# Other prices in a build-time scheduler's clock, and a sample's cached keys loaded in transposed form

## The chip, the cores and the metric

The kernel runs on one core of a Trainium2 chip. A core has five engines with instruction streams of their own: TensorE (PE, matrix products; its weight loads, PEld, overlap with them), VectorE (DVE), ScalarE (ACT), GpSimd (POOL) and SyncE (SP), which here issues every DMA. Each engine runs its stream in the order in which it was built, and waits on semaphores where it needs another's result. Matrix products are written to PSUM, everything else lies in SBUF, and DMAs move data between SBUF and device memory (DRAM). The metric is the device time of one execution in microseconds (us); lower is better.

## What is computed

One layer of a streaming encoder, in fp32, for 2048 frames of a new stream ("prompt") and 64 frames of a running one ("sample") with 4096 cached keys and values:

```python
h = rmsnorm(x, norm_g) @ w_in                     # 1024 -> 6144 columns
qa, ka, va, za, qb, kb, vb, zb, ga, gb = split(h)
qa = rmsnorm(qa.reshape(B, T, 4, 2, 64), qn_g)     # q and k: RMS norm per 64 columns
ka = rmsnorm(ka.reshape(B, T, 4, 2, 64), kn_g)
# branch A, differential attention; cache: (1, 1, 4096, 4 heads, 2, 64)
s = einsum('bqhcd,bkhcd->bhcqk', q, k) * 64 ** -0.5 - slopes * dist   # then the chunk mask
p = softmax(s);  a = p[:, :, 0] - lam * p[:, :, 1];  oa = a @ v
# branch B: retention, 4 heads, chunks of 64, a state carried on
m = sigmoid(ga) * ((rmsnorm(oa) * silu(za)) @ w_oa) + sigmoid(gb) * ((rmsnorm(ob) * silu(zb)) @ w_ob)
y = x + m @ w_out
```

For the sample, the keys are the cached ones followed by the 64 new ones. Outputs are y, the new k and v, and the retention states.

## The kernel before

**Products in three parts.** An fp32 operand is split in a high part rounded to fp32r (an ACT copy) and a low part (operand less high part, a DVE or POOL subtraction). A product is then three matmuls: high with high, high with low, low with high. In `mm_group` (L385) these are the matmuls of the input projection.

**Two streams of work.** `w_stream` makes the projections in two halves of 1024 prompt frames, the first with the sample's 64. Column groups of 256 columns follow each other. For each, `w_load` and `w_split` bring and split the weights (L355 on ACT, L362 on POOL), and `natural` (for v, k and q) runs one group of 24 matmuls for each tile of 128 frames into a PSUM tile `mm` (two buffers), then starts a task for what follows. For q and k that task is `fin_qk`: ACT copies the tile to `raw` (L418) and squares it into a `tlo` buffer (L419), DVE sums the squares (L424) and makes the mean (L426), ACT and DVE make the reciprocal root (`rsqrt_small`, L220 to L230), DVE multiplies `raw` (L434, and L438 for k), PE transposes the result (L451), ACT and DVE split it (L461 to L467), and DMAs store it. `raw`, `thi` and `tlo` have two buffers each. The other columns (`transposed`) are evacuated by `fin_t` (L551).

`z_stream` does attention and retention on what is stored. In `attn_head`, `qk_block` makes scores (L725, L726) and adds the bias on DVE (L734), `softmax` takes exponentials on ACT (L764) and combines the two rows on DVE (L785), and `at_pv` transposes the rows on PE (L832), splits them (L845, L847) and multiplies by v (L810 to L812). Between the two halves comes `sample_attn`. For each head and each 512 cached keys, it takes a loaded tile `kn`, has PE transpose it in four pieces into the PSUM tile `at` (L922), splits it (L933 on ACT, L935 on DVE) into `ath` and `atl`, and runs three matmuls (L892 to L894). The loader `s_loader` queues eight key tiles (`K`, four buffers) and nine value tiles (`V`, four buffers) for each head. After both streams, `out_stream` makes the output products (L1303 to L1305, L1368 to L1370).

**The planner.** All these functions are generators. While the kernel is built, `loop` resumes whichever is ready with the best priority, and what it then emits goes to the ends of the engines' streams; so the order on PE, ACT, DVE and the DMA queue is fixed by this loop. It keeps a clock for each engine. `P(cycles)` moves PE's, which is also the loop's present time; `A(n)`, `V(n)` and `G(n)` add an operation of n elements to ACT's, DVE's and POOL's and return when its result is there (`LAT`, 250 ns, later); `ld` does it for DMAs (bytes/300 ns + 2600 ns). A generator that yields a time is resumed when PE's clock has come there, one that yields a function when this is true. `take` and `give` hand out buffers with the times at which they come free. The clock decides only the order; on the chip the semaphores hold whatever was placed too early. The prices before the change are these:

```python
self.pe += cycles / 2.4 + 2.5                                  # P
self.act = max(self.act, ready) + 0.9 * n + 60 + extra         # A
self.dve = max(self.dve, ready) + rate * n + 65                # V, rate 1.05
self.pool = max(self.pool, ready) + 2.4 * n + 100              # G
```

Of the kernel before, what the change touches and what calls it, by code (L numbers as in the profile page):

```python
# [8 lines left out]
F32 = mybir.dt.float32  # L9
# [12 lines left out]
PAST = 4096  # L22
# [32 lines left out]
class Hybrid:  # L55
# [55 lines left out]
        self.res[tag].free += [t] * k  # L111

    def P(self, cycles):
        self.pe += cycles / 2.4 + 2.5
        return self.pe + LAT

    def A(self, n, ready=0.0, extra=0.0):
        self.act = max(self.act, ready) + 0.9 * n + 60 + extra
        return self.act + LAT

    def V(self, n, ready=0.0, rate=1.05):
        self.dve = max(self.dve, ready) + rate * n + 65
        return self.dve + LAT

    def G(self, n, ready=0.0):
# [148 lines left out]
    def x_norm(self, j, xt, jk, gn, t, tg, r, seg, col, left):  # L274
        nc = self.nc
        yield t
        ss, ms, y = (self.sp.tile([128, 1], F32, tag=k, name=k)[:r] for k in ("x_ss", "x_ms", "x_y"))
        nc.scalar.activation(jk[:r], xt, AF.Square, accum_out=ss)
        t = self.A(1024, self.pe, 270)
        yield t  # L280
        nc.scalar.activation(y, ss, AF.Ln, scale=1.0 / D, bias=self.epst[:r])
        nc.scalar.activation(y, y, AF.Exp, scale=-0.5)
        self.A(1, t, 140)
        t2 = self.A(1, 0, 140)
        nc.vector.tensor_scalar(ms, ss, 1.0 / D, EPS, op0=ALU.mult, op1=ALU.add)
        self.V(1, t)
        yield t2
        nc.vector.scalar_tensor_tensor(out=ms, in0=y, scalar=y, in1=ms, op0=ALU.mult, op1=ALU.mult)
        nc.vector.tensor_scalar(ms, ms, -0.5, 1.5, op0=ALU.mult, op1=ALU.add)
        nc.vector.tensor_mul(y, y, ms)  # L290
        for _ in range(3):
            t = self.V(100, t2)
        if tg > self.pe:
            yield tg
        nc.vector.scalar_tensor_tensor(out=xt, in0=xt, scalar=y, in1=gn[:r], op0=ALU.mult, op1=ALU.mult)
        self.xq[j] = (xt, self.V(1150, t), r, seg, col)
        left[0] -= 1

    def x_tile(self, j):
# [561 lines left out]
    def sample_attn(self):  # L861
        nc = self.nc
# [8 lines left out]
        for h in range(4):  # L871
            yield from self.take("q")
            qt = self.sb(ap, [128, 4, 256], "q", dt=F32R)
            qq = [qt[:, j, 0:128] for j in range(2)]
            for j in range(2):
                nc.vector.memset(qq[j].bitcast(F32), 0.0)
                t = self.V(128)
            yield t
            for j in range(2):
                for c in range(2):  # L880
                    tq = self.ld(qq[j][64 * c:64 * c + 64, 64 * c:64 * c + 64].bitcast(F32),
                                 self.qT[j][h, 64 * c:64 * c + 64, T:TT], 1 << 14)
            yield from self.take("row", 4)
            units = [self.row() for _ in range(4)]
            tail = sp.tile([128, 64], F32, tag="s_tail", name="s_tail", bufs=2)
            accs = sp.tile([128, 16], F32, tag="s_acc", name="s_acc", bufs=3)

            def mms(m, n, kh, kl, t):
                yield max(t, tq, tb)
                yield from self.take("s")  # L890
                ps = self.psum("s")[:, :n]
                nc.tensor.matmul(ps, qq[0], kh, start=True, stop=False)  # L892
                nc.tensor.matmul(ps, qq[0], kl, start=False, stop=False)
                nc.tensor.matmul(ps, qq[1], kh, start=False, stop=True)  # L894
                for _ in range(3):
                    t = self.P(max(n, 256))
                self.give("ath", t)
                self.give("atl", t)
                acc = accs[:, m:m + 1]
                out = units[m // 2][:, (m % 2) * 512:(m % 2) * 512 + 512] if m < 8 else tail  # L900
                tab = base[:, 0:512] if m < 8 else base[:, 512:576]
                nc.vector.tensor_tensor_reduce(
                    out=out, in0=ps, in1=tab, scale=-SLOPES[h], scalar=3.0e38,
                    op0=ALU.add, op1=ALU.min, accum_out=acc)
                t = self.V(n, t)
                if m < 7:
                    nc.vector.tensor_scalar_add(acc, acc, 512.0 * (7 - m) * SLOPES[h])
                    self.V(1)
                self.give("s", t)
                yield self.pe  # L910

            todo = None
            for m in range(9):
                n = 512 if m < 8 else 64
                if m < 8:
                    yield lambda: len(self.kns) > 0
                    kn, t = self.kns.pop(0)
                    yield t
                    yield from self.take("at")
                    tp = self.psum("at")  # L920
                    for k in range(4):
                        nc.tensor.transpose(tp[:, 128 * k:128 * k + 128], kn[:, k, :], self.ident)  # L922
                        t = self.P(256)
                    self.give("K", t)
                if todo is not None and not self.has("ath", "atl"):
                    yield from mms(*todo)
                    todo = None
                yield from self.take("ath")
                yield from self.take("atl")
                kh = self.sb(ap, [128, 512], "ath", dt=F32R)[:, :n]  # L930
                kl = self.sb(ap, [128, 512], "atl", dt=F32R)[:, :n]
                if m < 8:
                    nc.scalar.copy(kh, tp)  # L933
                    t = self.A(512, t)
                    nc.vector.tensor_sub(kl, tp, kh.bitcast(F32))  # L935
                    t = self.V(512, t)
                    self.give("at", t)
                else:
                    self.ld(kh.bitcast(F32), self.kT[0][h, :, T:TT], 1 << 15)
                    t = self.ld(kl.bitcast(F32), self.kT[1][h, :, T:TT], 1 << 15)  # L940
                yield self.pe
                if todo is not None:
                    yield from mms(*todo)
                todo = (m, n, kh, kl, t)
            yield from mms(*todo)
            self.give("q", self.pe + LAT)
            mx = sp.tile([128, 9], F32, tag="s_mx", name="s_mx", bufs=3)
            nc.vector.tensor_reduce(mx[:, 7:8], accs[:, :9], axis=AX.X, op=ALU.min)
            t = self.V(16, t)
            for m in range(7):  # L950
                nc.vector.tensor_scalar_add(mx[:, m:m + 1], mx[:, 7:8], -512.0 * (7 - m) * SLOPES[h])
                t = self.V(1)
            yield t
            lp = sp.tile([128, 16], F32, tag="s_lp", name="s_lp", bufs=3)
            nc.scalar.activation(tail, tail, AF.Exp, bias=mx[:, 7:8], scale=-1.0, accum_out=lp[:, 8:9])
            self.A(64, t, 220)
            te = []
            for m in range(8):
                u = units[m // 2][:, (m % 2) * 512:(m % 2) * 512 + 512]
                nc.scalar.activation(u, u, AF.Exp, bias=mx[:, m:m + 1], scale=-1.0, accum_out=lp[:, m:m + 1])  # L960
                te.append(self.A(512, t, 220))
            self.spawn(self.sample_pv(h, units, tail, te, lp, oall), 2, "z")
# [14 lines left out]
    def s_loader(self):  # L977
        for h in range(4):
            for m in range(8):
                yield from self.take("K")  # L980
                kn = self.sb(self.ap, [128, 4, 128], "K", "kn")
                t = self.ld(kn, self.i["cache_k_diff"][0, 0, 512 * m:512 * m + 512, h]
                            .rearrange("(t p) c d -> p t (c d)", p=128), 1 << 18)
                self.kns.append((kn, t))
                yield self.pe
            for m in range(9):
                yield from self.take("V")
                vc = self.sb(self.ap, [128, 4, 128], "V", "vc")
                if m < 8:
                    t = self.ld(vc, self.i["cache_v_diff"][0, 0, 512 * m:512 * m + 512, h]  # L990
                                .rearrange("(t p) e -> p t e", p=128), 1 << 18)
                else:
                    t = self.ld(vc[:64, 0, :], self.vsN[:, 128 * h:128 * h + 128], 1 << 15)
                self.vcs.append((vc, t))
                yield self.pe
# [596 lines left out]
```

## Time and profile before

| | us |
|---|---|
| median of three runs | 2158.24 |
| lowest and highest of them | 2155.09, 2160.27 |
| the profiled execution | 2151.0 |
| its span, first to last instruction | 2149.2 |
| mean granted TensorE clock | 0.984 of full speed |

The profile is of one execution. A row by engine and stretch gives the stretch's length, the busy time of each engine with its count of instructions, the granted TensorE clock (PEclk, 1.00 is full speed), the busy share of the DMA engines and GB/s. A row of a group gives line, engine, operation, the tile written and the tiles read, shapes and count; then busy time, mean ns of one, the engine's idle time just before such instructions, and which instruction ended that idle time. A row of the list of waits gives who waited for whom, us in total, times, and the longest. Matmuls overlap in the array, so a matmul's own duration is longer than the distance from one start to the next.

### The profile page before, as it was taken

The page shows a single profiled execution, that of the slowest core. Times are in us where ns is not written, and L with a number is a line of the kernel's source. Part 1 is how long each engine was busy: PE and PEld are TensorE (multiplying, and loading weights), DVE is VectorE, ACT ScalarE, POOL GpSimd, SP SyncE. Part 2 cuts the span into 40 slices and gives each one's busy share as a digit, 9 for nine tenths or more (in the row PEclk, how much of TensorE's full clock was granted, in tenths as well). Part 3 has the DMA queues.
Part 4 walks back from the last instruction along what each step waited for, and adds up shares of the span by engine and source line. Part 5 has one row for each costly group of instructions (what it writes and reads, how often), then busy time and mean ns, then how long its engine had stood idle before and what let it go on. Part 6 is the DMA issues. An engine that isn't in the chain of part 4 may idle for free.

```text
span 2149.2 us, 36945 instructions
## 1 busy us (share of the span) xinstructions
PE 2050.0 (95%) x13152; PEld 1853.5 (86%) x13152; DVE 1011.6 (47%) x2957; ACT 1006.9 (47%) x2349; POOL 462.6 (22%) x428
## 2 busy tenths in 40 slices
PE   7978999999999999988989999999999978999999
PEld 6977899989899999978879988888888867998897
DVE  6265856544311200455886756624642335454442
ACT  5333766644434422534765656644654334333221
POOL 1111112110122421110211121233123423222210
PEclk8999999999999999999999999999999989999999
DMA  6654444346545542455343252453233545444431
GB/s 206 189 144 124 136 137 128 112 122 171 156 120 133 159 140 84 130 152 152 94 133 110 70 147 87 136 165 94 64 96 115 172 144 185 134 143 146 135 115 60
DMA packets 363145, 281.66 MB, mean 131 GB/s; under 512 B 67408, under 2 KB 342480, under 8 KB 362960
## 3 DMA queue, kind: packets, MB, share of 16 engines
q1 hardware_dynamic: 362960, 279.30, 43.9%
q8 instruction: 104, 1.70, 0.3%
q14 instruction: 81, 0.66, 0.1%
HBM read 187.71 MB, written 91.49 MB: 130 GB/s over the span
## 4 chain that ended last, share of the span: by engine, by line
PE 48%; DVE 2%; DMA 1%; ACT 1%; issue 1%; SPq 0%; POOL 0%; POOLq 0%; DVEq 0%; ACTq 0%
PE mm L385 20%; PE at L1368 3%; PE at L1370 3%; PE at L1369 3%; PE at L832 2%; PE s L725 2%; PE s L726 2%; PE s L1304 1%; PE s L1303 1%; PE mm L1304 1%; PE mm L1303 1%; PE mm L1305 1%; PE s L1305 1%; PE pv L812 1%; PE pv L811 1%; PE pv L810 1%
## 5 line engine op out<-in xcount | busy, mean ns | idle before, releaser
L385 PE MATMUL mm<-xh,wh 128*128 128x512 f32 (+2 forms) x1280 | 466.2, 364 | 3.4 <-ACT ev L551 2.4
L385 PE MATMUL mm<-xh,wl 128*128 128x512 f32 (+2 forms) x1280 | 452.2, 353 | 0.3 <-POOL wl L362 0.3
L385 PE MATMUL mm<-xl,wh 128*128 128x512 f32 (+2 forms) x1280 | 451.8, 353 | 0.0
L362 POOL TENSOR_TENSOR wl<-ws,wh 128x512 fp32r<-128x512 f32 x190 | 252.0, 1346 | 771.6 <-ACT wh L355 562.9
L385 PE MATMUL mm<-wh,xh 128*128 128x256 f32 x1088 | 320.9, 295 | 11.8 <-ACT sq L419 6.9
L385 PE MATMUL mm<-wl,xh 128*128 128x256 f32 x1088 | 311.0, 286 | 1.1 <-POOL wl L362 0.8
L385 PE MATMUL mm<-wh,xl 128*128 128x256 f32 x1088 | 310.6, 285 | 0.2 <-DVE xl L317 0.2
L385 PEld LDWEIGHTS mm<-xh,wh 128*128 128x128 f32 x1280 | 241.9, 189 | 36.2 <-issue 3.4
L385 PEld LDWEIGHTS mm<-xl,wh 128*128 128x128 f32 x1280 | 242.0, 189 | 31.8 <-issue 3.4
L385 PEld LDWEIGHTS mm<-xh,wl 128*128 128x128 f32 x1280 | 241.4, 189 | 31.7 <-POOL wl L362 0.8
L385 PEld LDWEIGHTS mm<-wh,xh 128*128 128x128 f32 x1088 | 207.9, 191 | 19.1 <-ACT sq L419 9.9
L385 PEld LDWEIGHTS mm<-wl,xh 128*128 128x128 f32 x1088 | 208.2, 191 | 4.3 <-POOL wl L362 1.2
L385 PEld LDWEIGHTS mm<-wh,xl 128*128 128x128 f32 x1088 | 207.7, 191 | 0.4 <-DVE xl L317 0.4
L551 ACT COPY ev<-mm 128x512 f32<-128x512 f32 x140 | 71.3, 510 | 278.4 <-PE mm L385 230.3
L847 DVE TENSOR_TENSOR atl<-at,ath 128x512 fp32r<-128x512 f32 (+1 forms) x144 | 93.9, 660 | 145.3 <-ACT ath L845 145.0
L764 ACT ACTIVATE row<-row,a_mx 128x1024 f32<-128x1024 f32 (+7 forms) x160 | 153.3, 962 | 15.3 <-DVE a_mx L744 15.3
L734 DVE CUSTOM_DVE_ANT_0 row<-s,dfar 128x512 f32<-128x512 f32 (+2 forms) x192 | 117.8, 631 | 62.0 <-PE s L726 52.6
L845 ACT CAST ath<-at 128x512 fp32r<-128x512 f32 (+1 forms) x144 | 79.5, 562 | 112.2 <-PE at L832 111.6
L355 ACT CAST wh<-ws 128x512 fp32r<-128x512 f32 x192 | 116.1, 619 | 27.4 <-PE mm L385 21.7
L725 PE MATMUL s<-K,q 128*128 128x512 f32 (+3 forms) x320 | 122.8, 388 | 5.3 <-DVE a_acc L734 5.2
L609 POOL TENSOR_TENSOR r_y<-r_y,r_sq 128x256 f32<-128x256 f32 x33 | 29.5, 894 | 426.6 <-DVE r_sq L606 368.2
L726 PE MATMUL s<-K,q 128*128 128x512 f32 (+3 forms) x320 | 116.3, 365 | 0.0
(202 smaller groups left out, 4199.0 us busy)
## 6 DMA issues: line engine op xcount, KB each, us to landing
ws<-in_w_in_dram SPq DMA_DIRECT2D x192, 256.0 KB, 3.0
q<-qT SPq DMA_DIRECT2D x128, 128.0 KB, 2.9
V<-vN SPq DMA_DIRECT2D x24, 512.0 KB, 5.1
K<-kT SPq DMA_DIRECT2D x48, 256.0 KB, 3.8
gt<-gaT SPq DMA_DIRECT2D x64, 132.0 KB, 2.1
gt<-gbT SPq DMA_DIRECT2D x64, 132.0 KB, 2.2
xt<-in_x_prompt_dram SPq DMA_DIRECT2D x16, 512.0 KB, 5.1
kn<-in_cache_k_diff_dram SPq DMA_DIRECT2D x32, 256.0 KB, 3.5
```

The costliest lines, as they stand in the source:

```text
L355: nc.scalar.copy(h, st)
L362: nc.gpsimd.tensor_sub(l, st, h.bitcast(F32))
L385: nc.tensor.matmul(ps, p, q, start=c == 0 and i == 0, stop=c == KC - 1 and i == 2)
L551: nc.scalar.copy(ev, ps)
L725: nc.tensor.matmul(ps, q1s, kk, start=True, stop=False)
L726: nc.tensor.matmul(ps, q2s, kk, start=False, stop=True)
L734: nc.vector.tensor_tensor_reduce(out=units[k0 // 1024][:, k0 % 1024:k0 % 1024 + n], in0=ps, in1=tab, scale=-SLOPES[h], scalar=3.0e38, op0= ...
L764: nc.scalar.activation(u, u, AF.Exp, bias=mx, scale=-1.0, accum_out=lp[:, k:k + 1])
L845: nc.scalar.copy(ah[:, :w], at[:, :w])
L847: nc.vector.tensor_sub(al[:, :w], at[:, :w], ah[:, :w].bitcast(F32))
L1368: nc.tensor.matmul(ps, h, wh[:, nsl], start=ct == 0, stop=False)
L1369: nc.tensor.matmul(ps, h, wl[:, nsl], start=False, stop=False)
```

## The change

The prices of PE, ACT and DVE in the clock are changed, with the `extra` amounts and element counts in `x_norm` that stood beside the old ones. POOL's price, the DMAs' and `LAT` stay. The cached keys come to the kernel in a second layout, made by the host before the launch (head, channel, key): a tile of 512 keys is loaded as 128 partitions of 512 consecutive values, and is split from SBUF. The four transposes, the `at` tile and its give and take fall away; `K` is given back after the subtraction instead of after the transposes.

```diff
@@ P, A, V
-        self.pe += cycles / 2.4 + 2.5
+        self.pe += cycles / 2.4 + 13.0
...
-        self.act = max(self.act, ready) + 0.9 * n + 60 + extra
+        self.act = max(self.act, ready) + 0.84 * n + 165 + extra
...
-        self.dve = max(self.dve, ready) + rate * n + 65
+        self.dve = max(self.dve, ready) + rate * n + 155
@@ x_norm
-        t = self.A(1024, self.pe, 270)
+        t = self.A(1024, self.pe, 190)
...
-        self.A(1, t, 140)
-        t2 = self.A(1, 0, 140)
+        self.A(1, t, 40)
+        t2 = self.A(1, 0, 40)
...
-            t = self.V(100, t2)
+            t = self.V(20, t2)
...
-        self.xq[j] = (xt, self.V(1150, t), r, seg, col)
+        self.xq[j] = (xt, self.V(1100, t), r, seg, col)
@@ sample_attn
                     yield t
-                    yield from self.take("at")
-                    tp = self.psum("at")
-                    for k in range(4):
-                        nc.tensor.transpose(tp[:, 128 * k:128 * k + 128], kn[:, k, :], self.ident)
-                        t = self.P(256)
-                    self.give("K", t)
...
-                    nc.scalar.copy(kh, tp)
+                    nc.scalar.copy(kh, kn)
                     t = self.A(512, t)
-                    nc.vector.tensor_sub(kl, tp, kh.bitcast(F32))
+                    nc.vector.tensor_sub(kl, kn, kh.bitcast(F32))
                     t = self.V(512, t)
-                    self.give("at", t)
+                    self.give("K", t)
@@ s_loader
-                kn = self.sb(self.ap, [128, 4, 128], "K", "kn")
-                t = self.ld(kn, self.i["cache_k_diff"][0, 0, 512 * m:512 * m + 512, h]
-                            .rearrange("(t p) c d -> p t (c d)", p=128), 1 << 18)
+                kn = self.sb(self.ap, [128, 512], "K", "kn")
+                t = self.ld(kn, self.i["cache_k_T"][h, :, 512 * m:512 * m + 512], 1 << 18)
@@ kernel
+    k = given.pop("cache_k_diff")[0, 0]
+    given["cache_k_T"] = np.ascontiguousarray(k.transpose(1, 2, 3, 0).reshape(4, 128, PAST))
```

## The prediction

> **What bounds the kernel now.** First the page's busy times, then busy time by stretch of the span.
>
> ```profile
> span 2149.2 us, 36945 instructions
> PE 2050.0 (95%) x13152; PEld 1853.5 (86%) x13152; DVE 1011.6 (47%) x2957; ACT 1006.9 (47%) x2349; POOL 462.6 (22%) x428
> ...
> core 0: us, PE busy (x) PEld busy (x) DVE busy (x) ACT busy (x) POOL busy (x), PEclk, DMA share, GB/s
> 0.00:60.00 60.00, 46.07 (x311) 43.15 (x312) 34.35 (x89) 32.77 (x80) 5.64 (x9) 0.86 0.61 196
> 90.00:180.00 90.00, 71.04 (x539) 67.93 (x538) 52.66 (x179) 31.05 (x110) 13.47 (x11) 0.94 0.49 140
> 180.00:260.00 80.00, 72.21 (x543) 65.95 (x542) 59.41 (x246) 47.74 (x141) 11.48 (x9) 1.00 0.46 127
> 260.00:880.00 620.00, 615.41 (x4102) 566.18 (x4102) 207.93 (x628) 282.64 (x637) 132.28 (x110) 1.00 0.47 133
> 880.00:1000.00 120.00, 105.32 (x820) 100.43 (x819) 62.49 (x190) 50.99 (x147) 20.28 (x16) 0.99 0.51 151
> 1000.00:1150.00 150.00, 135.66 (x970) 126.35 (x969) 120.45 (x378) 96.93 (x233) 19.43 (x15) 0.95 0.41 119
> 1150.00:1735.00 585.00, 585.00 (x3270) 508.73 (x3269) 282.80 (x737) 316.08 (x625) 143.53 (x115) 1.00 0.37 112
> 1735.00:1800.00 65.00, 46.97 (x252) 39.95 (x251) 37.96 (x95) 36.35 (x95) 28.88 (x37) 0.82 0.62 193
> ```
>
> TensorE (PE) bounds it, without a break from 260 to 880 and from 1150 to 1735. PE is idle (length less busy) 13.9 us at the start, 18.0 us in 1735 to 1800, and 19.0 + 7.8 + 14.7 + 14.3 = 55.8 us in the four stretches of the q/k projections, two for each half; in the second of each, attention runs beside them. There the granted clock (the third number from the end) costs PE a further 90 x 0.06 + 120 x 0.01 + 150 x 0.05 = 14.1 us of work not done; in the two full stretches it is 1.00. So 69.9 us are open to a better order. Who is waited for: L451's group on PE in these four stretches, and from the list of waits the wait of the matmuls themselves:
>
> ```profile
> L451 PE MATMUL tp<-ident,raw 128*128 128x128 f32 (+1 forms) x38 | 7.7, 285 | 17.0 <-DVE raw L438 12.1 <-DVE raw L434 3.9 <-DVE tlo L467 0.8
> L451 PE MATMUL tp<-ident,raw 128*128 128x128 f32 (+1 forms) x34 | 6.6, 276 | 4.2 <-DVE raw L434 1.7 <-DVE r_sq L603 1.5 <-DVE tlo L462 0.8
> L451 PE MATMUL tp<-ident,raw 128*128 128x128 f32 x32 | 6.5, 284 | 10.0 <-DVE raw L438 5.9 <-DVE raw L434 2.7 <-DVE tlo L462 0.8
> L451 PE MATMUL tp<-ident,raw 128*128 128x128 f32 x32 | 6.6, 290 | 8.5 <-DVE raw L434 4.8 <-DVE tlo L467 2.2 <-DVE raw L438 1.2
> ...
> PE mm L385 <- ACT sq L419: 6.9, 11, 1.0
> ```
>
> The transposes of the normalised q/k tiles (L451) stand behind 17.0 + 4.2 + 10.0 + 8.5 = 39.7 us of the 55.8 us: PE's stream is fixed when the program is built, and the planner put them where VectorE (DVE) had not finished `raw`.
>
> **The planner's clock.** What a 256-column matmul takes start to start, and what the other engines take:
>
> ```profile
> 1158.14 0.28 PE L385 MATMUL mm<-wh,xh 128*128 128x256 f32 x1
> 1158.26 0.28 PE L385 MATMUL mm<-wl,xh 128*128 128x256 f32 x1
> ...
> L847 DVE TENSOR_TENSOR atl<-at,ath 128x512 fp32r<-128x512 f32 x112 | 76.2, 690 | 116.3 <-ACT ath L845 116.0
> L434 DVE TENSOR_TENSOR raw<-raw,sm_y 128x256 f32<-128x256 f32 x64 | 27.2, 425 | 2.3
> L228 DVE TENSOR_TENSOR sm_y<-sm_y,qscale 128x4 f32<-128x4 f32 x32 | 5.0, 155 | 0.0
> L845 ACT CAST ath<-at 128x512 fp32r<-128x512 f32 x112 | 64.3, 586 | 99.9 <-PE at L832 99.3 <-PE s L894 0.3
> L418 ACT COPY raw<-mm 128x256 f32<-128x256 f32 x64 | 23.6, 368 | 17.2 <-PE mm L385 8.5 <-issue 4.6 <-DMA out_k_prompt_dram<-raw 4.1
> L220 ACT ACTIVATE sm_y<-ms 128x4 f32<-128x4 f32 x64 | 13.1, 204 | 39.8 <-DVE ms L426 39.8
> L764 ACT ACTIVATE row<-row,a_mx 128x1024 f32<-128x1024 f32 x80 | 91.7, 1147 | 10.8 <-DVE a_mx L744 10.8
> L764 ACT ACTIVATION_READ_ACCUMULATOR row<-row,a_mx 128x1 f32 x160 | 30.2, 189 | 0.0
> ```
>
> The matmul takes 0.12 us. The old price is 256/2.4 + 2.5 = 109 ns, the new one 120. DVE at 512, 256 and 4 elements takes 690, 425 and 155 ns; the old prices are 603, 334 and 69, the new ones 693, 424 and 159. ScalarE (ACT) at 512 and 256 takes 586 and 368; old 521 and 290, new 595 and 380. So the small operations were priced at half or less, and the new prices are right there.
>
> In `fin_qk` one key tile's path from the end of its matmul group to its transposes is two ACT copies, two DVE operations, two small ACT ones, four small and two 256-wide DVE ones and five times 250 ns of latency. By the old prices that sums to 3.3 us of the planner's clock, 3.6 us of real matmuls (x 120/109); by the new ones 4.4 us. DVE has four 256-wide and five small operations for each key tile, priced 1.7 us before and 2.5 now, most of the 3.1 us that PE needs (24 x 0.12 + 2 x 0.11), so queues form in the plan too. The order of the two built programs, each matmul counted at its pace from the rows above (transposes below), shows it. I took the 43 tiles of the column groups that run without attention beside them: k, k, q of the first half, k, q of the second. The mean distance from a group's end to its transposes goes from 5.2 to 6.3 us, and tiles with under 5.3 us from 24 to 2. In the 25 later tiles, mixed with attention, the means go from about 11 to 13. What the path needs on the chip (the timeline's evacuation and last multiply of two neighbouring tiles):
>
> ```profile
> 117.04 0.38 ACT L418 COPY raw<-mm 128x256 f32<-128x256 f32 x1
> 120.08 0.36 ACT L418 COPY raw<-mm 128x256 f32<-128x256 f32 x1
> 120.13 0.42 DVE L438 TENSOR_TENSOR raw<-raw,gk 128x256 f32<-128x256 f32 x1
> 126.39 0.43 DVE L438 TENSOR_TENSOR raw<-raw,gk 128x256 f32<-128x256 f32 x1
> ```
>
> The first needs 3.5 us (117.04 to 120.55), the second, beside weight casts, 6.7 us (120.08 to 126.82). A distance of 5.2 us holds the first, 6.3 us holds nearly both.
>
> **The sum.** (1) L451's 39.7 us idle: 27.0 in the unmixed stretches, 12.7 in the mixed. The first falls by four fifths (2 tiles of 24 stay short, and some that need 6.7 us), the second by a third, as its distances grow by a sixth: 22 + 4 = 26 us. Bounds: all 39.7, or a loss of 10, if the longer-held `raw` and `tlo` buffers (two each) make the evacuation late and the wait goes to the matmuls (ACT sq L419, 6.9 us now, doubling and more). I add 3 us for that. (2) The clock: as it is at 1.00 wherever PE has no gaps, I let it come back in the same share as the gaps, 26/39.7: 9 of 14.1 us; bounds 0 and 14.1. (3) The start and the change of stage at 1735: PE's order there is the same but for a few transposes, and the start's long gap waits for an x tile at the same place in the DMA queue. 0, bounds -5 and +5.
>
> (4) The cached keys' transposes:
>
> ```profile
> 1054.60 0.87 PE at L832 x8
> ...
> L922 PE MATMUL at<-ident,kn 128*128 128x128 f32 x128 | 18.9, 274 | 0.0
> L933 ACT CAST ath<-at 128x512 fp32r<-128x512 f32 x32 | 18.5, 588 | 31.9 <-PE at L922 31.2 <-DVE atl L847 0.7
> L935 DVE TENSOR_TENSOR atl<-at,ath 128x512 fp32r<-128x512 f32 x32 | 22.0, 688 | 15.1 <-ACT ath L933 15.1
> L355 ACT CAST wh<-ws 128x512 fp32r<-128x512 f32 x192 | 116.1, 619 | 27.4 <-PE mm L385 21.7 <-DMA ws<-in_w_in_dram 2.1 <-issue 1.6
> ...
> kn<-in_cache_k_diff_dram SPq DMA_DIRECT2D x32, 256.0 KB, 3.5
> ```
>
> 128 transposes at 0.87/8 = 0.109 us are 14.0 us, all in 440 to 583, where PE has no idle time to lose: 14 us off the end. The copy now reads SBUF as the cast L355 does, 619 for 588, 32 times, 1.0 us beside matmuls; DVE's subtraction keeps its 688, as L434 with both inputs in SBUF lies on the line of L847. The load has the same 256 KB, one row of 2 KB per partition for four of 512 bytes: 3.5 us as now, or a little less. The copy waits for that landing itself instead of through a transpose. The `K` buffer is given back after the subtraction, two operations later, about 1.3 us; with four buffers and other matmuls to run, I cost both at nothing. If that cover is gone, 32 x 1.3 = 42 us.
>
> Against the change speaks this: the subtraction now has two inputs in SBUF, like L225, which can be held up, while POOL's split takes 1.29 us:
>
> ```profile
> L225 DVE TENSOR_TENSOR sm_t<-sm_t,ms x68: 153/163/1270, 93.8 to 1138.9; 128x4 f32<-128x4 f32 x64, 64x4 f32<-64x4 f32 x4
> L362 POOL TENSOR_TENSOR wl<-ws,wh x190: 1259/1292/2272, 9.5 to 1716.3; 128x512 fp32r<-128x512 f32 x190
> ```
>
> POOL is busy 132 of 620 us there, a fifth, so 6 or 7 of 32 meet it and lose up to 1.1 us: at most 8 us of DVE, which has 208 busy of 620. The Trainium skill, "SBUF — State Buffer", section "Who interferes with whom", says that an instruction of VectorE with two SBUF inputs contends with a GpSimd one that reads SBUF, and that the one which comes second is blocked for the whole other. L225's maximum agrees. By that rule alone the sum would be 8 us less at worst, if DVE set the pace.
>
> Sum: 26 + 9 - 3 + 14 = 46 us. The profiled execution took 2151.0 us around its span, so it would take 2105; it lies below the three runs shown (2155.1 to 2160.3), so I take the 46 us from their median: 2158.2 - 46 = 2112 us. I give this case alone 2090 to 2135.
>
> **The rivals.** *The waits only move*: the two `raw` buffers and DVE are short, not the order. For it: DVE is busy 120 of 150 us in the last stretch, and its operations queue behind each other. Against it: in the unmixed stretches it is busy 53 of 90 and 62 of 120. Then the transposes alone count: 2158 - 14 = 2144. *All of it goes*: every idle and throttled microsecond of the four stretches, 70 + 14: 2074. Against it are attention's own DVE chains in the mixed ones.
>
> *Slower: prices left short.* The planner's clock now passes 10% faster per matmul, and whatever was not raised as much comes 10% sooner in matmuls. DMA's fixed 2600 ns, POOL's price and the latency stay, and the exponentials lose: 1024 elements cost 1201, that is 1320 real, now 1245, against 1147 + 189 = 1336 measured. Who would wait: PE, at attention's transposes and the sample's products, in the two stretches that are full now.
>
> ```profile
> V<-vN SPq DMA_DIRECT2D x24, 512.0 KB, 5.1
> K<-kT SPq DMA_DIRECT2D x48, 256.0 KB, 3.8
> ```
>
> Of each, one tenth of the price: 190 splits x 0.15, 96 loads of cached keys and values and V x 0.35 to 0.4, 160 exponentials x 0.09: 28 + 35 + 14 = 77 us. It decides once over 46 of these reach PE; in full, with the gain kept, 2158 - 46 + 77 = 2189. For it: V lands in 5.1 us and is priced at 4.3. Against it: loads and splits are made many tiles ahead. *It does not do what it says*: the order changes, but stalls come back elsewhere in the two full stretches, where thousands of matmuls are re-ordered, and eat the 14 too: about 2158.
>
> **How the numbers follow.** Forecast 0.55 (2112), waits only move 0.17 (2144), all goes 0.13 (2074), no net change 0.05 (2158), slower 0.10 (2189). The range, 2078 to 2148, leaves out the slower case, no change and half of the largest gain. 0.2% (4.3 us) is about what a measurement tells from no change. Faster holds the first three: 0.85; within it 0.05; slower 0.10.
>
> **What would show it.** Right: no L922, PE with 128 fewer instructions; L451's idle time under 16 us; granted clock 0.98 or more in the four stretches; 260 to 880 some 14 us shorter; waits for ACT sq L419 under 10 us. Wrong: L451's waits gone but L385 idle by as much behind sq or raw; L832, L810 or L892 waiting for DVE, ACT or DMA by over 10 us; PE idle in what are now the full stretches.

## The result and the profile after

| | us |
|---|---|
| before, median of four runs | 2157.95 (2155.09 to 2160.27) |
| after, median of four runs | 2141.07 (2139.46 to 2143.21) |
| ratio, 95% interval | 0.9923 [0.9906, 0.994] |
| profiled execution after, its span | 2143.21, 2141.3 |

The change is worth 16.9 us where 46 were forecast. Up to L922 the lines keep their numbers; behind it they fall by 6, and from `s_loader` on by 7. First the page of the kernel after, its head and its busy times, then (second fence) busy times by stretch, with the stretches cut where the work changes as in the view of before.

```profile
span 2141.3 us, 36714 instructions
...
PE 2044.0 (95%) x13024; PEld 1853.6 (87%) x13024; DVE 1027.2 (48%) x2957; ACT 1009.3 (47%) x2349; POOL 459.8 (21%) x428
```

```profile
0.00:60.00 60.00, 45.13 (x302) 42.43 (x303) 35.05 (x88) 32.20 (x78) 6.25 (x8) 0.89 0.63 195
...
90.00:180.00 90.00, 77.39 (x592) 75.05 (x591) 55.81 (x184) 34.20 (x118) 15.68 (x12) 0.92 0.51 145
180.00:260.00 80.00, 68.09 (x492) 62.52 (x491) 56.64 (x222) 44.77 (x131) 12.25 (x10) 0.96 0.44 120
260.00:865.00 605.00, 603.03 (x3987) 556.86 (x3988) 210.20 (x637) 280.79 (x634) 131.55 (x109) 1.00 0.49 137
865.00:985.00 120.00, 103.26 (x771) 98.96 (x770) 67.21 (x191) 51.64 (x149) 20.51 (x16) 0.94 0.50 144
985.00:1135.00 150.00, 136.00 (x982) 127.42 (x982) 119.11 (x378) 97.38 (x234) 18.88 (x15) 0.95 0.41 116
...
1720.00:1790.00 70.00, 53.02 (x278) 45.84 (x277) 37.99 (x90) 35.83 (x92) 28.13 (x36) 0.80 0.56 169
```

The 128 transposes are gone from PE's count, and the first full stretch, with the sample's attention in it, is 605 us long instead of 620. The four q/k stretches are as long as they were, 440 us together. PE is idle in them for 12.6 + 11.9 + 16.7 + 14.0 = 55.2 us (55.8 before), and the granted clock, the third number from the end, now costs 90 x 0.08 + 80 x 0.04 + 120 x 0.06 + 150 x 0.05 = 25.1 us (14.1 before). Much of these 11 us goes with the choice of the profiled executions. The profiled one of before had a mean clock of 0.984 and is the fastest on record; 31 others, run beside the experiments, had 0.979 to 0.985, 0.982 on average. The four of after had 0.978 (the profiled one, the slowest of them), 0.981, 0.982 and 0.982. At these averages the clock costs 39 us over the span before and 41 after. So, too, the two profiled spans differ by only 7.9 us, and the medians by 16.9. So the transposes' 14 us stayed, and the re-ordering gave nothing. Who is waited for has changed, though. The transposes' groups on PE in the same four stretches, after:

```profile
L451 PE MATMUL tp<-ident,raw 128*128 128x128 f32 (+1 forms) x40 | 8.1, 287 | 7.3 <-DVE raw L438 7.2
L451 PE MATMUL tp<-ident,raw 128*128 128x128 f32 (+1 forms) x28 | 5.6, 283 | 3.0 <-DVE raw L434 3.0
L451 PE MATMUL tp<-ident,raw 128*128 128x128 f32 x28 | 5.8, 292 | 6.3 <-DVE raw L438 3.5 <-DVE raw L434 2.6
L451 PE MATMUL tp<-ident,raw 128*128 128x128 f32 x34 | 7.2, 296 | 6.2 <-DVE raw L434 4.3 <-DVE r_sq L603 1.1 <-DVE tlo L467 0.7
```

And the list of PE's waits after (us in total, times, longest), the rows that bear on the prediction:

```profile
PE mm L385 <- ACT sq L419: 25.1, 27, 1.8
PE tp L451 <- DVE raw L438: 10.7, 3, 3.6
PE tp L451 <- DVE raw L434: 9.9, 6, 2.7
PE tp L309 <- DVE xl L317: 8.0, 3, 4.8
...
PE at L832 <- DVE row L785: 0.3, 1, 0.3
```

The idle time ahead of L451 fell from 39.7 to 7.3 + 3.0 + 6.3 + 6.2 = 22.8 us, that is by 16.9. The projection matmuls' wait for the evacuation (ACT sq L419, the last reader of their `mm` tile) rose from 6.9 to 25.1 us, by 18.2. The same time changed places. Why ACT is late shows in the timeline (start, duration, engine, line; in brackets the engine's idle time before and what ended it):

```profile
139.27 0.42 SPq L130 DMA_DIRECT2D out_k_prompt_dram<-raw  x1
...
139.49 0.38 PE L451 MATMUL tp<-ident,raw 128*128 128x128 f32 x2
...
139.91 0.37 ACT L466 CAST thi<-tp 128x256 fp32r<-128x256 f32 x1 [1.48 <-PE tp L451]
...
142.53 0.37 ACT L418 COPY raw<-mm 128x256 f32<-128x256 f32 x1 [1.91 <-DMA out_k_prompt_dram<-raw]
142.80 0.39 ACT L419 ACTIVATE sq<-mm 128x256 f32<-128x256 f32 x1
...
143.24 0.39 PE L385 MATMUL mm<-wh,xh 128*128 128x256 f32 x1 [1.22 <-ACT sq L419]
```

A `raw` buffer comes free when its tile is transposed and, for k, its store has landed. Here the transposes end at 139.87, but the store, issued at 139.27, holds the buffer until ACT may start at 142.53. ACT stands for 1.91 us, the matmuls behind it for 1.22. Over the whole span, ACT's copy to `raw` stood for that store 9.8 us in 9 places. That is the view of line L418's instructions, after:

```profile
  DMA out_k_prompt_dram<-raw: 9.8, 9
```

Before it was 4.9 us in 3 places. ACT is also held by the order of its own stream: L466 above waited 1.48 us for PE's transposes, and everything behind it on ACT waited too. What L451 still waits for is partly something else, the longest wait of 3.6 us:

```profile
118.04 5.32 POOL L362 TENSOR_TENSOR wl<-ws,wh 128x512 fp32r<-128x512 f32 x4 [22.68 <-PE mm L385]
118.08 1.26 DVE L230 TENSOR_TENSOR sm_y<-sm_y,sm_t 128x4 f32<-128x4 f32 x1
...
119.38 1.45 DVE L434 TENSOR_TENSOR raw<-raw,sm_y 128x256 f32<-128x256 f32 x1
...
120.86 1.37 DVE L438 TENSOR_TENSOR raw<-raw,gk 128x256 f32<-128x256 f32 x1
...
122.38 0.66 PE L451 MATMUL tp<-ident,raw 128*128 128x128 f32 x2 [3.61 <-DVE raw L438]
...
122.59 0.80 DVE L426 TENSOR_SCALAR ms<-ms 128x4 f32<-128x4 f32 x1
```

While POOL runs four weight splits in a row, three DVE operations with both inputs in SBUF take 1.26, 1.45 and 1.37 us, where L230 otherwise takes 0.16 and the other two 0.42. The chain of one tile grows by 3.1 us at a place where the plan has no room for it. The other two of the three waits for L438 are made the same way: beside the runs of splits at 155.80 and 937.04 us the three operations take the same times, to 0.01 us.

### The profile page after: what moved, and what is told of

Read it like the earlier page. It is cut to its first block, busy times and chain, and to the rows that moved or that the text cites. A ratio compares the mean times of both kernels' runs of the same rounds, so it can differ in the third digit from the quotient of the medians.

```text
span 2141.3 us, 36714 instructions
## 1 busy us (share of the span) xinstructions
PE 2044.0 (95%) x13024; PEld 1853.6 (87%) x13024; DVE 1027.2 (48%) x2957; ACT 1009.3 (47%) x2349; POOL 459.8 (21%) x428
## 4 chain that ended last, share of the span: by engine, by line
PE 85%; DVE 5%; DMA 4%; ACT 3%; issue 1%; POOL 0%; SPq 0%; POOLq 0%; ACTq 0%; DVEq 0%
PE mm L385 48%; PE at L1361 3%; PE s L725 3%; PE s L726 3%; PE at L1363 3%; PE at L1362 3%; PE at L832 3%; PE pv L812 2%; PE pv L811 1%; PE pv L810 1%; PE mm L1296 1%; PE s L1297 1%; PE mm L1298 1%; PE mm L1297 1%; PE s L1298 1%
## 5 line engine op out<-in xcount | busy, mean ns | idle before, releaser
L385 PE MATMUL mm<-xh,wh 128*128 128x512 f32 (+2 forms) x1280 | 465.2, 363 | 2.5 <-ACT ev L551 2.5
L385 PE MATMUL mm<-xl,wh 128*128 128x512 f32 (+2 forms) x1280 | 452.2, 353 | 0.0
L385 PE MATMUL mm<-xh,wl 128*128 128x512 f32 (+2 forms) x1280 | 452.2, 353 | 0.0
L385 PE MATMUL mm<-wh,xh 128*128 128x256 f32 x1088 | 325.8, 299 | 27.3 <-ACT sq L419 25.1
L385 PE MATMUL mm<-wl,xh 128*128 128x256 f32 x1088 | 315.4, 290 | 1.3 <-POOL wl L362 1.0
L385 PE MATMUL mm<-wh,xl 128*128 128x256 f32 x1088 | 315.0, 289 | 0.2 <-DVE xl L317 0.2
L385 PEld LDWEIGHTS mm<-xh,wh 128*128 128x128 f32 x1280 | 242.3, 189 | 36.6 <-issue 3.6
L385 PEld LDWEIGHTS mm<-xl,wh 128*128 128x128 f32 x1280 | 242.5, 189 | 32.8 <-issue 3.6
L385 PEld LDWEIGHTS mm<-xh,wl 128*128 128x128 f32 x1280 | 242.0, 189 | 31.1
L385 PEld LDWEIGHTS mm<-wh,xh 128*128 128x128 f32 x1088 | 212.7, 196 | 38.3 <-ACT sq L419 32.3
L385 PEld LDWEIGHTS mm<-wl,xh 128*128 128x128 f32 x1088 | 213.1, 196 | 4.5 <-POOL wl L362 1.2
L385 PEld LDWEIGHTS mm<-wh,xl 128*128 128x128 f32 x1088 | 212.6, 195 | 0.4 <-DVE xl L317 0.4
L355 ACT CAST wh<-ws 128x512 fp32r<-128x512 f32 x192 | 117.0, 619 | 34.5 <-PE mm L385 30.1
```

The lines of the kernel that those rows point to most:

```text
L355: nc.scalar.copy(h, st)
L385: nc.tensor.matmul(ps, p, q, start=c == 0 and i == 0, stop=c == KC - 1 and i == 2)
```

## The experiments

Three theories stood for the missing 29 us. A: the prices do nothing for the time, since the two `raw` buffers (and the two `tlo`) bound the distance between a matmul group and its transposes. B: the prices are right and the gain is there, but POOL's runs of splits, or the order of ACT's stream, take it back. C: the prices cost somewhere else what they gain here. All ratios are against the kernel before, run beside each on the same chip (medians 2155.5 to 2155.8 us), with 95% intervals.

**The two halves of the change apart.** `clock_only` has the new prices and loads, transposes and splits the cached keys as before:

```diff
@@ sample_attn, s_loader, kernel: as before the change
+                    yield from self.take("at")
+                    tp = self.psum("at")
+                    for k in range(4):
+                        nc.tensor.transpose(tp[:, 128 * k:128 * k + 128], kn[:, k, :], self.ident)
...
-    given["cache_k_T"] = np.ascontiguousarray(k.transpose(1, 2, 3, 0).reshape(4, 128, PAST))
```

> The new prices of PE, ACT and DVE alone; the cached keys are still transposed on PE. If the waits only moved from the transposes L451 to the evacuations L419 (the theory), the prices are worth little: 0 to -5 us, with L451's idle time near 22 us (38 in the kernel before) and the matmuls' wait for L419 near 25 us (7 before). If the prices bring most of the gain (rival), -10 us or more.

`host_only` has the transposed keys and the old prices:

```diff
@@ P, A, V, x_norm: as before the change
-        self.pe += cycles / 2.4 + 13.0
+        self.pe += cycles / 2.4 + 2.5
...
-        self.act = max(self.act, ready) + 0.84 * n + 165 + extra
+        self.act = max(self.act, ready) + 0.9 * n + 60 + extra
...
-        self.dve = max(self.dve, ready) + rate * n + 155
+        self.dve = max(self.dve, ready) + rate * n + 65
```

> The transposed cached keys alone, with the old prices. Theory: the 128 transposes at 0.109 us come off in full, -12 to -16 us, and L451's idle time stays at 36 to 40 us. Rival (a part of the 14 us is covered by other work): -5 us or less.

Measured: `clock_only` 1.0003 [0.9992, 1.0014], 2158.5 us; `host_only` 0.9899 [0.9883, 0.9916], 2135.8 us. PE's waits in `clock_only`:

```profile
PE mm L385 <- ACT sq L419: 25.6, 28, 1.8
PE tp L451 <- DVE raw L438: 10.8, 3, 3.6
```

and in `host_only`:

```profile
PE tp L451 <- DVE raw L438: 19.3, 16, 2.0
PE tp L451 <- DVE raw L434: 11.6, 8, 4.5
PE mm L385 <- ACT sq L419: 9.5, 11, 1.8
```

The new prices move the wait from L451 to L419 with or without the transposed keys (L451's idle time is 22.8 us in `clock_only` and 38.0 in `host_only`), and by themselves they are worth nothing that can be measured. The transposed keys alone give 20 us by the median, above the 12 to 16 expected; that this is more than the whole change gives isn't shown, as the two intervals overlap. Their own 128 transposes explain 14.0 of it. In the two profiles, the span fell by 15.3 us (2149.2 to 2133.9) and PE's busy time by 14.3. The profiled execution of before, 2151.0 us, is the fastest of all its runs, with a mean clock of 0.984 against 0.982 in `host_only`: 0.002 of 2134 us, some 4 us, may be why the profiles show less than the medians. What the transposed keys give beyond the 14.0 stays open.

**The buffers.** To make room for a third `raw` buffer, the weights' staging tiles `ws` go from 4 to 3, and that was run alone too:

```diff
@@ ws3
-        "ws": 4, "w": 12, "r_o": 1, "r_sq": 1, "r_y": 1, "state": 2,
+        "ws": 3, "w": 12, "r_o": 1, "r_sq": 1, "r_y": 1, "state": 2,
@@ raw3_ws3, beside it
-BUFS = {"raw": 2, "thi": 2, "tlo": 2, "ev": 2, "q": 2, "K": 4, "V": 4, "ath": 2, "atl": 2,
+BUFS = {"raw": 3, "thi": 2, "tlo": 2, "ev": 2, "q": 2, "K": 4, "V": 4, "ath": 2, "atl": 2,
```

> The changed kernel with three weight staging buffers for four and nothing else, to tell what that costs. Both theories: within 4 us of the changed kernel, or slower, as weights come later; the matmuls' wait for L419 stays near 25 us.

> The changed kernel with three raw buffers in place of two; the space comes from the weight staging (ws, three for four). If raw's two buffers, held until the store has landed, make the evacuations late, the matmuls' wait for L419 falls from 25 to under 8 us and the time by 10 to 25 us below the changed kernel. If DVE, held up by POOL's weight splits, sets the pace (rival), L451's waits of 2.5 to 3.6 us stay, and the time changes by less than 6 us.

Measured: `ws3` 0.9884 [0.9865, 0.9903], 2132.8 us; `raw3_ws3` 0.9737 [0.9719, 0.9755], 2101.4 us. PE's waits in `ws3`:

```profile
PE mm L385 <- ACT sq L419: 29.8, 30, 1.9
PE tp L451 <- DVE raw L434: 10.3, 5, 5.0
...
PE tp L451 <- DVE raw L438: 6.8, 6, 1.8
```

and the first of `raw3_ws3`:

```profile
PE mm L385 <- ACT sq L419: 16.8, 14, 2.9
```

The third `raw` buffer is worth 31 us, takes 13 us off the wait for L419, and L451's idle time falls from 19.9 to 5.1 us. That is theory A in kind, not in size: the time fell by more than the 10 to 25 us expected below the change, and the wait for L419 didn't fall under 8. That `ws3` is itself 8 us faster than the change was foreseen by none; by the mean clocks of their executions (0.983 and 0.981) 4 to 5 of the 8 are clock. A smaller stock of staged weights leaves shorter runs of splits, but that was only argued. What ACT's square stands for in `raw3_ws3`, from the view of line L419's instructions:

```profile
  DMA kT<-tlo: 5.0, 4
  DMA qT<-tlo: 3.3, 2
```

L419 writes into a `tlo` buffer, of which there are also two, each held until its store has landed. So a third of these, with the new prices (`raw3_tlo3`), and the third `raw` alone and both with the old prices (`old_raw3`, `old_raw3_tlo3`; `ws` 3 in all):

```diff
@@ raw3_tlo3, beside ws 3
-BUFS = {"raw": 2, "thi": 2, "tlo": 2, "ev": 2, "q": 2, "K": 4, "V": 4, "ath": 2, "atl": 2,
+BUFS = {"raw": 3, "thi": 2, "tlo": 3, "ev": 2, "q": 2, "K": 4, "V": 4, "ath": 2, "atl": 2,
@@ old_raw3 and old_raw3_tlo3, beside 3 raw, and 3 raw and 3 tlo: P, A, V, x_norm
-        self.pe += cycles / 2.4 + 13.0
+        self.pe += cycles / 2.4 + 2.5
...
```

> The changed kernel with three raw and three tlo buffers, ws three. The next buffer in the same row is tlo, which holds the squares and then the low part until it is stored: if it makes what is left of the matmuls' wait for L419 (16.8 us with three raw buffers alone), that falls under 9 us and the time to 0.966 to 0.971 of the kernel before. Rival (the wait is ACT's stream, in which L419 stands behind a split that waits for the transposes): no change, 0.972 to 0.976.

> Three raw buffers (ws three) and the transposed keys, with the old prices. Theory (two conditions: the transposes far enough behind, and buffers that allow it): the old prices put the transposes about 5 us behind whatever the buffers, so L451's idle time stays over 25 us and the time at 0.983 to 0.990 of the kernel before. Rival (the buffer alone gives it, the prices are worth nothing): 0.972 to 0.977 as with the new prices, L451's idle time under 12 us.

> Three raw and three tlo buffers, ws three, transposed keys, old prices. If the prices pay once the buffers let PE run ahead (theory), it is 8 to 20 us slower than with the new prices: 0.974 to 0.978 of the kernel before, PE waiting at L451 for 15 us or more. If the buffers alone give the gain (rival): 0.966 to 0.971.

Measured, all with the transposed keys:

| buffers | old prices | new prices |
|---|---|---|
| as in the change (`ws` 4) | 0.9899 [0.9883, 0.9916] | 0.9923 [0.9906, 0.994] |
| `raw` 3, `ws` 3 | 0.9795 [0.9776, 0.9814] | 0.9737 [0.9719, 0.9755] |
| `raw` 3, `tlo` 3, `ws` 3 | 0.9688 [0.9675, 0.9702] | 0.9685 [0.9669, 0.97] |

PE's waits in `old_raw3`:

```profile
PE tp L451 <- DVE tlo L467: 11.3, 12, 2.4
PE mm L385 <- ACT sq L419: 9.2, 11, 2.0
...
PE tp L451 <- DVE tlo L462: 6.7, 7, 2.0
```

In `raw3_tlo3`:

```profile
PE tp L451 <- DVE tlo L467: 6.4, 3, 3.2
PE mm L385 <- ACT sq L419: 6.4, 7, 1.3
...
PE mm L385 <- POOL wl L362: 0.3, 1, 0.3
```

and its q/k stretches, of which the last is shorter by 20 us than after the change:

```profile
90.00:180.00 90.00, 83.38 (x686) 81.31 (x685) 64.42 (x221) 40.32 (x142) 14.17 (x12) 1.00 0.58 161
180.00:260.00 80.00, 73.48 (x568) 69.27 (x568) 61.41 (x231) 49.89 (x141) 10.02 (x10) 1.00 0.46 127
...
850.00:970.00 120.00, 115.95 (x944) 113.58 (x942) 72.73 (x226) 63.34 (x179) 24.69 (x19) 1.00 0.59 174
970.00:1100.00 130.00, 123.05 (x931) 118.68 (x932) 105.32 (x327) 85.56 (x203) 19.45 (x17) 0.97 0.41 116
```

With both buffers PE is idle there for 6.6 + 6.5 + 4.1 + 7.0 = 24.2 us, 31.0 less than after the change, and the clock costs 130 x 0.03 = 3.9 us, 21.2 less. Together that is 52.2 us, beside 55.5 by which the span is shorter (2141.3 to 2085.8). The sum is of two profiled executions and is good only to some us: the first full stretch has a clock of 0.99 there, a loss of 590 x 0.01 = 5.9 us that it leaves out, and by the mean clocks of all executions (0.981 and 0.988) the clock gives 16 us, not 21. It is the kind of gain that the prediction booked for the prices, and the buffers give it: at three `raw` and three `tlo` old and new prices can't be told apart. PE's idle time at L451 in `old_raw3_tlo3`, in the whole span:

```profile
L451 PE MATMUL tp<-ident,raw 128*128 128x128 f32 x136 | 26.9, 280 | 10.8 <-DVE raw L438 4.9 <-DVE raw L434 3.7 <-DVE tlo L462 1.5
```

The idea that the prices pay once the buffers are there, which `raw3_ws3` against `old_raw3` (11 us) had seemed to support, falls with this run. At the middle step, where `old_raw3` lay between its two forecasts, the prices differ, and by the two lists in where the wait stands: with the old order at L451, whose single `tp` tile is read last by the operation that writes `tlo` (L467, L462), with the new one at L419. The third `tlo` buffer takes most of both: 11.3 + 6.7 us at L451 become 1.9 with the old prices, and 16.8 at L419 become 6.4 with the new.

A third buffer also changes the plan, since `take` counts the buffers. From the order of PE's instructions in the traces, at the prediction's pace and for its 43 tiles, the mean distance from a group's end to its transposes is 4.8 us before, 5.8 after the change (5.2 and 6.3 by the prediction's count), 8.5 in `raw3_ws3`, 7.5 in `old_raw3`, 7.2 in `raw3_tlo3` and 6.2 in `old_raw3_tlo3`. So with three of each the old prices, too, place the transposes far enough behind. That the distance alone doesn't make the gain shows in `old_raw3_tlo3` against the changed kernel: 6.2 and 5.8 us, nearly the same, but 2088 and 2141 us, with 1.9 and 25.1 us of waits for L419. What a third buffer would give with the order left as it is, no run shows.

**POOL's runs and ACT's order.** `spaced` makes the planner wait 3 us of its clock after each split; `late_hi` puts ACT's copy of the transposed tile into the streams only after the transposes' planned end, so that ACT doesn't stand at it:

```diff
@@ spaced: w_split
             self.wq.append((h, l, t))
+            yield self.pe + 3000
@@ late_hi: fin_qk
             self.give("raw", max(t, ts))
+            yield t
             yield from self.take("thi")
```

> The changed kernel; the planner lets 3 us of its clock pass after each weight split, so that POOL's splits no longer come four in a row. If DVE held up by these runs of splits makes L451's longest waits, the three waits of 3.5 us for L438 go, L438's longest falls little (one split still blocks) and the time falls by 4 to 10 us below the changed kernel. If the buffers alone make the rest: within 3 us.

> The changed kernel; fin_qk lets the planner's clock reach the end of its transposes before it emits the split (L461, L466) behind them, so that other ACT work is placed ahead of it. If ACT's stream (evacuation behind a split that waits for PE) makes the waits for L419, they fall from 25 to under 12 us and the time by 6 to 15 us. If the buffers make them: 20 us or more stay, and the time is within 4 us of the changed kernel.

Measured: `spaced` 0.99 [0.9883, 0.9918], 2136.5 us; `late_hi` 0.9863 [0.9843, 0.9882], 2125.4 us. PE's waits in `spaced`, whose line numbers are one higher from L366 on:

```profile
PE mm L386 <- ACT sq L420: 32.0, 29, 1.9
...
PE tp L452 <- DVE raw L439: 8.4, 8, 1.9
...
PE mm L386 <- POOL wl L362: 3.9, 6, 1.0
```

and in `late_hi`:

```profile
PE tp L451 <- DVE raw L438: 20.1, 8, 5.0
PE mm L385 <- ACT sq L419: 11.6, 12, 1.8
```

Spacing the splits takes the longest wait for L438 from 3.6 to 1.9 us, and the wait for the evacuation grows by 7 us instead. The 5 us by which the time falls below the change lie within overlapping intervals, so this stays undecided. `late_hi` gains 13 us over the change, so ACT's order has a part in it. But it too moves the wait, back to L451: with two buffers, one end or the other of the chain is waited for.

**Both on top of the buffers.** `r3t3_late`, `r3t3_spaced` and `r3t3_both` are `raw3_tlo3` with the edits above:

```diff
@@ w_split: r3t3_spaced, r3t3_both
+            yield self.pe + 3000
@@ fin_qk: r3t3_late, r3t3_both
+            yield t
```

> Three raw and three tlo buffers, new prices, and the split emitted only when the planner's clock has passed its transposes. With the buffers there, the place of the split on ACT should matter little: within 6 us of three raw and tlo buffers without it (0.966 to 0.972). Rival (ACT's stream is a cause by itself): 0.961 to 0.965.

> Three raw and three tlo buffers, new prices, and 3 us of the planner's clock after each weight split. If runs of splits on POOL hold up DVE and so make the waits that are left at L451 (13 us), those fall under 8 us and the time by 3 to 8 us: 0.965 to 0.967. Rival (they are hidden by the longer distances): 0.968 to 0.971.

> Both of these with three raw and three tlo buffers. If the two are separate causes, their gains add: 0.960 to 0.965. If the waits only move again: 0.967 to 0.972.

Measured: 0.9672 [0.9658, 0.9687], 0.9727 [0.9714, 0.974] and 0.9664 [0.9651, 0.9677], that is 2085.5, 2096.7 and 2083.2 us. `r3t3_late` isn't distinguishable from `raw3_tlo3`: what ACT's order cost, the buffers take away too. `r3t3_spaced` is 8 us slower than `raw3_tlo3`, which no theory expected. In the list of its waits, matmuls wait for the splits themselves:

```profile
PE mm L386 <- POOL wl L362: 3.5, 7, 1.0
```

That is 3.5 us where `raw3_tlo3` has 0.3, and `spaced` had 3.9. Much of the 8 us lies in the first full stretch: from 260 to 850 us PE is idle for 8.9 us where it was 3.9, with waits of 1.3 us for the splits and 2.1 for ACT's casts of weights (L355). The rest is open. `r3t3_both` has the lowest median, but isn't told from `r3t3_late` or `raw3_tlo3`. All three are faster than both kernels: by 2.7 to 3.4% than before, and by 2.1 to 2.7% than the change (ratios of their medians to 2141).

## Why the prediction was wrong, point by point

**(1) L451's waits: the step that failed.** The prediction took 26 us for them and wrote, of a wait that goes to the matmuls, "I add 3 us for that". The waits did fall, by 16.9 us. The new wait was not 3 us but 18.2, the whole of it; the loss was named, with its place (ACT sq L419) and the buffers as its reason, and put at the edge of the bounds. Two of the prediction's own numbers pointed there. A group takes PE 3.1 us, so two `raw` buffers cover 6.2 us, and the new order holds a tile for 6.3 us from the group's end to its transposes on average (5.8 by the order in the trace), and k tiles until their store has landed besides. That is an argument from averages; what shows the cause is the runs above: the prices alone only move the wait, and third buffers take it away with old prices and new. One reading was incomplete, too. The path of 6.7 us, put down to weight casts, also holds L224 and L225 at 1.14 and 1.22 us where they else take 0.16, beside POOL's run of splits from 120.25 to 125.46: 2.0 us of the 6.7.

**(2) The clock.** Booked to come back with the gaps, 9 of 14.1 us. It didn't: the loss is 25.1 us in the profiled execution, with as many idle microseconds as before. How much of the 11 us more is the change's, the profiles can't say: by the averages of all executions given above, the clock's cost over the span rose by 2 us, which such averages don't tell from nothing. In `raw3_tlo3`, where idle time falls from 55.2 to 24.2, the granted clock is back at 1.00 in three stretches and 0.97 in the fourth, and its four executions have mean clocks of 0.987 to 0.989. So fewer gaps went with a higher clock, as assumed, and after the change there were no fewer. It is no fixed price for each microsecond of gaps: the same kernel, before, was granted 0.979 to 0.985.

**(3) Start and change of stage.** At the start, the wait for L317 grew from 2.0 to 8.0 us, but others fell (L285 from 7.7 to 3.4), and the idle time of the first 60 us went from 13.9 to 14.9 us. From 1720 to 1790 it is 17.0, from 18.0. Zero was right to a microsecond.

**(4) The transposes.** Right in place and size: 14.0 us forecast; the first full stretch is shorter by 15 (its ends are cut to 5 us), the span by 15.3 for this part alone. The copy from SBUF takes 621 ns, 619 forecast. The subtraction, from the rows of the kernel after by shape:

```profile
L929 DVE TENSOR_TENSOR atl<-kn,ath 128x512 fp32r<-128x512 f32 x32 | 24.1, 752 | 16.6 <-ACT ath L927 13.1 <-DMA kn<-in_cache_k_T_dram 3.2
```

Its mean is 752 ns instead of 688, 2.1 us in all, where up to 8 were allowed, and none of it reached PE: from 430 to 600 us its list of waits holds 0.4 us, for a load of values. By the Trainium skill, "SBUF — State Buffer", section "Who interferes with whom", of a VectorE instruction with two SBUF inputs and a GpSimd one that reads SBUF, the second is blocked for the whole of the first. The trace agrees in kind: in the run of splits shown above, each split takes 5.32/4 = 1.33 us, and the DVE operations beside it 1.26 to 1.45. The prediction applied it to the new subtraction, where it is harmless, and not to L434 and L438, which were there all along and which the chain waits for. In the trace of before L434 never took over 0.43 us, so its row gave no sign of it; L438's longest was 1.53.

**The rivals.** *The waits only move*, with 0.17 and 2144 us, is what happened (2141). Its ground, two `raw` buffers and DVE short, was right for the buffers. The argument against it, that DVE is busy for only 53 of 90 us, looked at an engine's share where the bound is how long a buffer is held. *Slower: prices left short* would have shown at L832, which waits 0.3 us, or in the two full stretches, which hold 2.0 and 1.1 us of idle time. That loads and splits were made far enough ahead fits this, but was not tried apart. *All goes* and *no change* are excluded by the interval, which for the change is 13 to 20 us of gain.

**What would show it.** Of the five signs for being right, L922's absence and the shorter stretch came true. L451's idle time (22.8, not under 16), the clock (0.92 to 0.96, not 0.98) and L419 (25.1, not under 10) did not, and the first of the signs for being wrong, L385 idle behind sq, did.

## What to carry to other kernels

Before crediting a planner for putting a consumer later, compare the new distance with what the buffers on the way hold: buffers times the period of the producer, and a store that must land counts in the hold. Here the wait moved up the chain by as much as it fell, and what helped was a third buffer. Before measuring prices anew, ask whether a buffer makes the waits that they are to remove: old and new prices gave the same time as soon as three of each were there, in an order that the buffer counts had changed as well. And before reading a few microseconds of clock out of one profile, look at the clocks of the other executions.

## What was not expected of the hardware

Beside a run of four POOL splits, DVE operations with two SBUF inputs took about as long as one split, even one of 4 elements (1.26 us for 0.16). Two inputs aren't needed for it: L426, with one input in SBUF, took 0.80 us for 0.17 in the run shown, up to the run's end, while the reduction L424 just before it kept its 0.41. Fewer staged weights were faster: `ws` 3 instead of 4 gave 8 us (0.9884 against 0.9923, with intervals that just don't meet), although PE's waits for L419, L438 and L434 sum to 46.9 us there and to 45.7 after the change.
